# Cross attention on Trainium2: the decode sample's scores of all four heads issued together

## The chip, the core and the metric

The kernel runs on one core of a Trainium2 chip. The metric is the device time of one launch in microseconds (us). Three runs of the kernel before took 992.42, 989.74 and 990.02 us; their median is 990.02 us.

Engines are named as in the profile: PE is TensorE's matrix products and PEld its weight loads, DVE is VectorE, ACT is ScalarE, POOL is GpSimd, SP is SyncE, which issues most of the loads.

## The reference, cut to what matters

One step of a two-layer encoder, for a prompt of 256 tokens and a decode sample of 32 tokens that share the weights. Each layer has a mixer, a cross attention into 256 memory tokens, and an MLP. In the cross attention the prompt uses keys and values projected from its memory; the sample uses cached ones. There are four heads of width 256.

```python
def cross_attend(hn, k, v, w_q, q_gain, w_o):
    b, t, _ = hn.shape
    q = rmsnorm((hn @ w_q).reshape(b, t, N_HEADS_X, HEAD_DIM_X), q_gain)
    s = jnp.einsum('bqhd,bkhd->bhqk', q, k) * (HEAD_DIM_X ** -0.5)
    p = jax.nn.softmax(s, axis=-1).astype(v.dtype)
    o = jnp.einsum('bhqk,bkhd->bqhd', p, v)
    return o.reshape(b, t, -1) @ w_o
```

For the sample that is, per head, a product of 32 queries with 256 keys over a width of 256, which is two products over 128 partitions each.

## The kernel before

All 288 tokens (256 of the prompt, 32 of the sample) are kept feature-major: features on partitions, tokens on columns. Weights stream from HBM in chunks of 1024 x 256 (`load_chunk`). SP loads half a chunk into one of four `raw` buffers; ACT (line 145, sometimes DVE, line 143) rounds it to a first part `wh`, and DVE or POOL (line 146) takes the rest `wl`. Each float32 product is then three products of such parts (lines 160 to 162), and a chunk has 48 of them for 288 columns.

`cross` (line 658) handles a layer's cross attention; the list `ORD_X` gives the order in which its steps are written: `s1 s2 s3 s0 v0 v1 S v2 v3`. A step `s` (`scores`, line 666) loads the head's cached keys `cmk` (line 668, two buffers in turn), projects the queries (`gemm2`), normalises them (`xnorm`: a column sum on PE at lines 329 and 330, `rx` on ACT, the query tile `xq` on DVE at line 343), and then issues two products for the sample (line 678): the 32 sample columns of `xq` are the weights, `cmk` moves through, and the result goes into 32 partitions of the bank `xs`, at the head's own group of 32 array columns (`tile_position=(0, 32 * hd)`). Behind them come the prompt's scores `sx` of the same head, their softmax (DVE lines 452 to 461, ACT line 458) and their transposes (line 697). A step `v` (`values`) projects memory values and multiplies them with the probabilities (`pox`). `S` (`sample`, line 718) takes the softmax of `xs` for all four heads at once and multiplies the cached values (line 729): eight products, two per head, again each head in its own group of 32 array columns, one behind the other.

The order on each engine is not the order of the text. A scheduler in the framework places every instruction when the kernel is built, by its own estimate of when its operands are ready, and each engine then works in that order. So the sample's two products of a head stand between products of weights that are ready anyway.

At the start POOL fills constants: `mones`, `mtri` and `bmask` are tiles of their own; DVE copies the mask into `smask` (line 272) and makes rounded copies `monesr` and `mtrir` (lines 275, 277) before its first split of the tokens (line 198). `scr` is a pool of scratch tiles, with eight buffers in turn under the tag `f`.

Of the kernel before, what the change touches and what calls it, by code (L numbers as in the profile page):

```python
# [14 lines left out]
P = 128  # L15
# [5 lines left out]
FB = 8  # L21
# [32 lines left out]
def body(ctx: ExitStack, tc: tile.TileContext, i: dict, o: dict):  # L54
# [18 lines left out]
    # four PSUM banks and the attentions' scratch change hands from phase to phase  # L73
# [30 lines left out]
    h = const.tile([P, KT, T], F32, name="h")  # L104

# [8 lines left out]
    # the array's clock rises after some microseconds of work, which can go by before the first data are there  # L114
# [5 lines left out]
    def load_chunk(ap, w=CW, split=2, before=None):  # L120
        # before: called with each row tile in turn, whose weights are then loaded on their own
        nk = KT // split
        ws = []
        for s in range(split):
            raw = wraw.tile([P, nk, w], F32, tag="raw", name="raw")
            if before is None:
                nc.sync.dma_start(out=raw, in_=ap[:, s * nk:(s + 1) * nk, :])
            nq = min(nk, NQ) if split > 1 else nk
            step = min(nq, R.step) if before is None else 1
            for k in range(0, nk, step):  # L130
                if k % nq == 0:
                    wh = wspl.tile([P, nq, w], F32R, tag="wh", name="wh")
                    wl = wspl.tile([P, nq, w], F32R, tag="wl", name="wl")
                    ws += [(wh[:, j, :], wl[:, j, :]) for j in range(nq)]
                r, src = slice(k % nq, k % nq + step), raw[:, k:k + step, :]
                if before is not None:
                    nc.sync.dma_start(out=src, in_=ap[:, s * nk + k:s * nk + k + 1, :])
                    before(s * nk + k)
                R.count += 1
                e = nc.gpsimd if R.count % R.pool_every == 0 and before is None else dve  # L140
                with ahead(HPS):
                    if R.dve_every and R.count % R.dve_every == 0 and before is None:
                        dve.tensor_copy(wh[:, r, :], src)
                    else:
                        act(wh[:, r, :], src, AF.Copy)  # L145
                    e.tensor_tensor(wl[:, r, :], src, wh[:, r, :].bitcast(F32), ALU.subtract)  # L146
        return ws
# [6 lines left out]
    def held():  # L154
        # products kept for later, when the engine would have nothing else to do
        return tc.issue_after(R.after) if R.after is not None else ExitStack()

    def mm3(out, lh, ll, rh, rl, first, last):
        # a float32 product from exact float32r parts
        mm(out, lh, rh, start=first, stop=False)  # L160
        mm(out, lh, rl, start=False, stop=False)  # L161
        return mm(out, ll, rh, start=False, stop=last)  # L162

    def gemm(tiles, ws, xh, xl, n=T, steps=GO):
        # the chunk's output tiles advance together, so that its first weights are free early
        for k0, k1 in zip((0,) + steps, steps + (KT,)):
            for out, cols in tiles:
                for k in range(k0, k1):
                    wh, wl = ws[k]
                    last_mm[0] = mm3(out, wh[:, cols], wl[:, cols], xh[:, k, 0:n], xl[:, k, 0:n],  # L170
                                     k == 0, k == KT - 1)
# [15 lines left out]
    class Norm:  # L187
        # (x * gain) in two exact parts, and the rows' 1 / rms, which commutes with the projection
# [11 lines left out]
        def rms(self, pool=()):  # L200
            # the squares of the row tiles in pool are summed by the Pool engine
            sums = {}
            for k in range(KT):
                hk, on = h[:, k, :], k in pool
                if on not in sums:
                    sq = sums[on] = scr.tile([P, T], F32, tag="ssum", name="ssum", bufs=2)
                else:
                    sq = scr.tile([P, T], F32, tag="f", bufs=FB, name="sq")
                if on:
                    nc.gpsimd.tensor_tensor(sq, hk, hk, ALU.mult)  # L210
                else:
                    act(sq, hk, AF.Square)
                if sq is not sums[on]:
                    (nc.gpsimd if on else dve).tensor_tensor(sums[on], sums[on], sq, ALU.add)
            ps = bank(R.m, "ps_rs")
            for n, on in enumerate(sums):
                mm(ps[:, 0:T], ones, sums[on], start=n == 0, stop=n == len(sums) - 1)
            rs = scr.tile([P, T], F32, tag="rs", name="rs")
            rstd_of(ps[:, 0:T], T, 1.0 / 1024, rs)
            return self.xh, self.xl, rs  # L220
# [9 lines left out]
    mones = const.tile([P, P], F32, name="mones")  # L230
    nc.gpsimd.memset(mones, -1.0)
# [8 lines left out]
    # -1 where key' >= key, for the suffix sums of the stick-breaking weights  # L240
    mtri = const.tile([P, P], F32, name="mtri")
    nc.gpsimd.affine_select(mtri, mones, pattern=[[-1, P]], compare_op=ALU.is_ge, fill=0.0,
                            base=0, channel_multiplier=1)
    # causal mask of the forgetting attention: prompt (last key tile) and sample (packed queries)
    bmask = const.tile([P, NP_], F32, name="bmask")
# [27 lines left out]
    # float32r holds 0 and 1 exactly  # L273
    mtrir = const.tile([P, P], F32R, name="mtrir")
    dve.tensor_copy(mtrir, mtri)
    monesr = const.tile([P, P], F32R, name="monesr")
    dve.tensor_copy(monesr, mones)
# [4 lines left out]
    # gains of the query-key norms; the queries' carry the attention scale, and a zero for the other head  # L282
# [40 lines left out]
    def sum_parts(ps, sel, sq, n):  # L323
        # column sums of float32 squares, exactly split in two float32r parts
        sh = scr.tile([P, T], F32R, tag="f", bufs=FB, name="sh")
        dve.tensor_copy(sh[:, 0:n], sq[:, 0:n])
        sl = scr.tile([P, T], F32R, tag="f", bufs=FB, name="sl")
        (nc.gpsimd if HNP else dve).tensor_tensor(sl[:, 0:n], sq[:, 0:n], sh[:, 0:n].bitcast(F32), ALU.subtract)
        mm(ps[:, 0:n], sel, sh[:, 0:n], start=True, stop=False)
        mm(ps[:, 0:n], sel, sl[:, 0:n], start=False, stop=True)  # L330
# [113 lines left out]
    def softmax_rows(s, bias, pr, ntile):  # L444
        # s: list of (scores, bias, probabilities) of 128 queries each; rows are normalised in place
# [17 lines left out]
    def pv_prompt(po, par, p, vt, pt0, pt1):  # L463
        # po: the pair's output features on partitions, prompt queries on columns
# [25 lines left out]
    def attend_ab(kind, g, qz, kT, vt, ck, cv, oh, ol, b1, b0, bsmp):  # L490
        kt0 = 4 * kind + 2 * g
        # sample: 4 heads x 32 queries on the partitions
# [54 lines left out]
    def softplus(zs, w, a):  # L547
        # max(z, 0) + ln(1 + exp(-|z|)); a list of score tiles side by side in w and a
# [13 lines left out]
    def below_diag(x, pattern):  # L562
        # keeps key < query: key on the partitions, query in the last pattern dimension
# [3 lines left out]
    def attend_c(g, qz, kT, vt, ck, cv, oh, ol):  # L567
        kt0 = 2 * g
        k_ = dict(start=False, skip_group_check=True)
        for p in range(2):  # L570
            # key tile 0: both heads' 256 queries; key tile 1: both heads' last 128 queries
# [45 lines left out]
        # sample: 4 heads x 32 queries on the columns, three key tiles  # L617
# [40 lines left out]
    def cross(layer, xh, xl, rs, mk, mh, ml):  # L658
        oh = spp.tile([P, KT, T], F32R, tag="sp", name="oh")
        ol = spp.tile([P, KT, T], F32R, tag="sp", name="ol")  # L660
        ss = bank(R.o, "xs")
# [4 lines left out]
        def scores(hd):  # L666
            cmk = R.ph.tile([P, 2, NP_], F32, tag="ck", name="cmk", bufs=2)
# [9 lines left out]
            for d in range(2):  # L677
                mm(ss[32 * hd:32 * hd + 32, 0:NP_], q[:, d, NP_:T], cmk[:, d, :], start=d == 0, stop=d == 1,  # L678
                   tile_position=(0, 32 * hd))
# [37 lines left out]
        # sample: 4 heads x 32 queries on the partitions  # L717
        def sample():
            pr = scr.tile([P, T], F32, tag="f", bufs=FB, name="prxs")
# [72 lines left out]
    # forget gates; the negated running sums go through DRAM to be read by all partitions  # L792
# [118 lines left out]
def _feat(a, np):  # L911
    # [tokens, features] -> [partition, feature tile, token]
# [4 lines left out]
def _tok(a, np):  # L917
    # [tokens, features] -> [partition, token tile, feature]
# [4 lines left out]
def _chunks(w, np):  # L923
    # [K, N] -> [N/256, 128, K/128, 256]
# [4 lines left out]
def _layout(x, np):  # L929
# [10 lines left out]
    # one row per query: the clipped-relative-position bias of its keys  # L940
# [21 lines left out]
    # [layer, out chunk, quarter, 128, 8, 256]  # L962
# [54 lines left out]
```

## Time and profile before

| | |
|---|---|
| runs | 992.42, 989.74, 990.02 us, median 990.02 |
| profiled execution, first to last instruction | 987.5 us |
| what the median has beyond that span | 2.5 us |
| PE, DVE, ACT, POOL busy | 976.4, 686.6, 541.3, 243.2 us |

The profile is one execution. Its own time by the clock of the runs is not listed beside its span; at the median, 2.5 us would lie around the span. Times of a row are counted from the span's first instruction. Matmuls overlap each other in the records: one that takes 0.29 us by its row starts 0.13 us behind the one before, so how much of PE's time a product costs is read from the starts of its neighbours.

### The profile page before, as it was taken

Reading aid. Unit: us, or ns where it says so; the run is one execution under the profiler, and the core shown is the slowest. Engines: PE = TensorE matmul, PEld = TensorE weight load, DVE = VectorE, ACT = ScalarE, POOL = GpSimd, SP = SyncE. Lnnn points to the kernel's source line nnn. Section 1 sums busy time; section 2 is a strip of 40 time slices with the busy share of each in tenths; the row PEclk is TensorE's granted clock in tenths of the full one; section 3 lists DMA queues with packets and bytes.
Section 4 is the critical chain, followed back from the end, with each engine's and each line's share of the span. In section 5 each row is a group of like instructions: output and inputs, shape, how many; then the busy total and the mean of one; then the engine's idle time right before and its main releaser. Section 6 shows DMA issues by size and latency. Waiting matters only on the chain.

```text
span 987.5 us, 19363 instructions
## 1 busy us (share of the span) xinstructions
PE 976.4 (99%) x7276; PEld 935.3 (95%) x7276; DVE 686.6 (70%) x1460; ACT 541.3 (55%) x1272; POOL 243.2 (25%) x267
## 2 busy tenths in 40 slices
PE   8999999999999999999999999999999999999998
PEld 8998888998999999999999888889999999999998
DVE  8778878678677767776786555668897766464643
ACT  5667566545456645454555657755454565453532
POOL 4311562211112211222122232233333211111111
PEclk8999999999999999999999999999999999999999
DMA  8554454654555555555565434246444455555552
GB/s 272 190 174 147 143 167 160 192 170 131 166 168 169 169 165 161 169 170 160 167 208 188 143 119 142 96 145 204 153 129 149 157 166 166 163 164 171 169 167 75
DMA packets 50702, 160.03 MB, mean 162 GB/s; under 512 B 6296, under 2 KB 12968, under 8 KB 50352
## 3 DMA queue, kind: packets, MB, share of 16 engines
q1 hardware_dynamic: 46864, 148.69, 47.2%
q0 software_dynamic: 2592, 8.92, 2.4%
q10 hardware_dynamic: 1152, 1.18, 0.4%
q8 instruction: 57, 0.93, 0.4%
q14 instruction: 37, 0.30, 0.1%
HBM read 148.65 MB, written 10.12 MB: 161 GB/s over the span
## 4 chain that ended last, share of the span: by engine, by line
PE 96%; DVE 1%; DMA 1%; ACT 0%; issue 0%; SPq 0%; DVEq 0%
PE g L160 27%; PE g L162 27%; PE g L161 27%; PE po L467 1%; PE xs L678 1%; DMA bsmp<-cd 1%; PE za L467 1%; PE za L584 1%; PE s L522 0%; PE zs L624 0%; PE za L605 0%; PE za L468 0%; PE sx L162 0%; SPq L849 0%; PE sx L161 0%
## 5 line engine op out<-in xcount | busy, mean ns | idle before, releaser
L145 ACT ACTIVATE wh<-raw 128x512 fp32r<-128x512 f32 (+3 forms) x561 | 279.4, 549 | 235.5 <-PE g L161 123.0
L146 DVE TENSOR_TENSOR wl<-raw,wh 128x512 fp32r<-128x512 f32 (+3 forms) x483 | 308.9, 673 | 112.2 <-ACT wh L145 106.3
L146 POOL TENSOR_TENSOR wl<-raw,wh 128x512 fp32r<-128x512 f32 (+2 forms) x141 | 175.0, 1242 | 556.1 <-ACT wh L145 465.6
L161 PE MATMUL g<-xl,wh 128*128 128x288 f32 (+1 forms) x1032 | 304.4, 297 | 2.3 <-DVE xl L198 2.3
L160 PE MATMUL g<-xh,wh 128*128 128x288 f32 (+1 forms) x1032 | 302.8, 298 | 1.1 <-ACT wh L145 0.7
L162 PE MATMUL g<-xh,wl 128*128 128x288 f32 (+1 forms) x1032 | 302.7, 298 | 0.0
L161 PEld LDWEIGHTS g<-xl,wh 128*128 128x128 f32 (+1 forms) x1032 | 193.8, 188 | 4.2 <-DVE xl L198 2.5
L162 PEld LDWEIGHTS g<-xh,wl 128*128 128x128 f32 (+1 forms) x1032 | 193.0, 188 | 3.6 <-issue 2.7
L160 PEld LDWEIGHTS g<-xh,wh 128*128 128x128 f32 (+1 forms) x1032 | 192.5, 188 | 2.7 <-ACT wh L145 0.8
L161 PE MATMUL g<-hl,wh 128*128 128x288 f32 x512 | 150.3, 295 | 0.0
L160 PE MATMUL g<-hh,wh 128*128 128x288 f32 x512 | 149.0, 295 | 0.0
L162 PE MATMUL g<-hh,wl 128*128 128x288 f32 x512 | 148.6, 294 | 0.0
L161 PEld LDWEIGHTS g<-hl,wh 128*128 128x128 f32 x512 | 96.1, 188 | 0.0
L162 PEld LDWEIGHTS g<-hh,wl 128*128 128x128 f32 x512 | 95.8, 188 | 0.0
L160 PEld LDWEIGHTS g<-hh,wh 128*128 128x128 f32 x512 | 95.4, 188 | 0.0
L161 PE MATMUL g<-ol,wh 128*128 128x288 f32 x256 | 75.0, 295 | 0.0
L160 PE MATMUL g<-oh,wh 128*128 128x288 f32 x256 | 73.9, 296 | 0.6 <-ACT oh L486 0.6
L162 PE MATMUL g<-oh,wl 128*128 128x288 f32 x256 | 73.9, 296 | 0.0
L774 DVE TENSOR_TENSOR h<-h,g 128x288 f32<-128x288 f32 x64 | 28.8, 449 | 29.0 <-PE g L162 28.9
L160 PEld LDWEIGHTS g<-oh,wh 128*128 128x128 f32 x256 | 47.4, 188 | 1.0 <-ACT oh L486 0.8
L162 PEld LDWEIGHTS g<-oh,wl 128*128 128x128 f32 x256 | 47.7, 188 | 0.6 <-issue 0.6
L161 PEld LDWEIGHTS g<-ol,wh 128*128 128x128 f32 x256 | 48.1, 188 | 0.0
(322 smaller groups left out, 1561.9 us busy)
## 6 DMA issues: line engine op xcount, KB each, us to landing
raw<-in_w_up_dram SPq DMA_DIRECT2D x64, 512.0 KB, 3.8
raw<-in_w_down_dram SPq DMA_DIRECT2D x64, 512.0 KB, 3.8
raw<-in_w_kv_dram SPq DMA_DIRECT2D x32, 512.0 KB, 3.9
raw<-in_sb_w_dram SPq DMA_DIRECT2D x24, 512.0 KB, 4.4
raw<-in_ab_w_dram SPq DMA_DIRECT2D x22, 512.0 KB, 4.9
raw<-in_w_q_dram SPq DMA_DIRECT2D x16, 512.0 KB, 4.5
raw<-in_w_o_dram SPq DMA_DIRECT2D x16, 512.0 KB, 4.1
raw<-in_ab_wo_dram SPq DMA_DIRECT2D x8, 512.0 KB, 4.1
```

The source lines that it names most:

```text
L145: act(wh[:, r, :], src, AF.Copy)
L146: e.tensor_tensor(wl[:, r, :], src, wh[:, r, :].bitcast(F32), ALU.subtract)
L160: mm(out, lh, rh, start=first, stop=False)
L161: mm(out, lh, rl, start=False, stop=False)
L162: return mm(out, ll, rh, start=False, stop=last)
L467: mm(dst[:, 0:NP_], vt[:, 0, cols], pt0, start=True, stop=False)
L584: mm(za2, x[:, 0:P], y, start=f_, stop=False, skip_group_check=True)
L678: mm(ss[32 * hd:32 * hd + 32, 0:NP_], q[:, d, NP_:T], cmk[:, d, :], start=d == 0, stop=d == 1, tile_position=(0, 32 * hd))
L774: dve.tensor_tensor(h[:, kt, :], h[:, kt, :], ps[:, 0:T], ALU.add)
```

## The change

`scores` no longer issues the sample's products. It copies the 32 sample columns of the head's query on POOL into `qsm`, a tile that holds all four heads. The cached keys have four buffers, so that all heads' keys stay. `sample` then issues the eight products, first half of all heads, then second half. The bank `xs` is taken there.

The two float32 constants `mones` and `mtri` and the mask `bmask` become scratch tiles, to make room; the later uses of `mones` and `mtri` read the rounded copies, which hold the same values. The many other lines of the diff only take comments away.

```diff
-    mones = const.tile([P, P], F32, name="mones")
-    nc.gpsimd.memset(mones, -1.0)
+    mones_ = scr.tile([P, T], F32, tag="f", bufs=FB, name="mones")[:, 0:P]
+    nc.gpsimd.memset(mones_, -1.0)
...
-    mtri = const.tile([P, P], F32, name="mtri")
+    mtri_ = scr.tile([P, T], F32, tag="f", bufs=FB, name="mtri")[:, 0:P]
...
-    bmask = const.tile([P, NP_], F32, name="bmask")
+    bmask = scr.tile([P, T], F32, tag="f", bufs=FB, name="bmask")[:, 0:NP_]
...
-    dve.tensor_copy(mtrir, mtri)
+    dve.tensor_copy(mtrir, mtri_)
+    mtri = mtrir.bitcast(F32)
...
     def cross(layer, xh, xl, rs, mk, mh, ml):
         oh = spp.tile([P, KT, T], F32R, tag="sp", name="oh")
         ol = spp.tile([P, KT, T], F32R, tag="sp", name="ol")
-        ss = bank(R.o, "xs")
+        qsm = R.ph.tile([P, 4, 2, NS], F32, tag="qsm", name="qsm")
+        cmks = {}
...
         def scores(hd):
-            cmk = R.ph.tile([P, 2, NP_], F32, tag="ck", name="cmk", bufs=2)
+            cmk = cmks[hd] = R.ph.tile([P, 2, NP_], F32, tag="ck", name="cmk", bufs=4)
...
             xnorm(t, T, xg[:, layer, :], q)
-            for d in range(2):
-                mm(ss[32 * hd:32 * hd + 32, 0:NP_], q[:, d, NP_:T], cmk[:, d, :], start=d == 0, stop=d == 1,
-                   tile_position=(0, 32 * hd))
+            nc.gpsimd.tensor_copy(qsm[:, hd, :, :], q[:, :, NP_:T])
...
         def sample():
+            ss = bank(R.o, "xs")
+            for d in range(2):
+                for hd in range(4):
+                    mm(ss[32 * hd:32 * hd + 32, 0:NP_], qsm[:, hd, d, :], cmks[hd][:, d, :], start=d == 0, stop=d == 1,
+                       tile_position=(0, 32 * hd))
```

In the changed kernel the copy is line 680, the eight products are line 724, the column sums 331 and 332, the loads of the keys 671. What the built order makes of it:

On PE in layer 0, before the change, around the two calls of head 1, the first head. The tiles `g` are weight products, `cmk_2815` is head 1's cached keys, `xq_2882` its query:

```order
L161 MATMUL g_3083<-xl_2749,wh_3077 128x288
L678 MATMUL xs_2812<-cmk_2815,xq_2882 32x256
L162 MATMUL g_3083<-xh_2748,wl_3078 128x288
L160 MATMUL g_3208<-xh_2748,wh_3197 128x288
L161 MATMUL g_3208<-xl_2749,wh_3197 128x288
L678 MATMUL xs_2812<-cmk_2815,xq_2882 32x256
L162 MATMUL g_3208<-xh_2748,wl_3198 128x288
L329 MATMUL ps_xn_3009<-sh_3015,onesr_244 128x288
```

Each of the 16 calls of the two layers stands alone like this: two to four wide products lie between the two calls of a head, and many more between heads.

On PE in layer 0 after the change, where the sample's scores stand now. `cmk_3190` belongs to head 0, `cmk_2815` to head 1, `cmk_2940` to head 2, `cmk_3065` to head 3; `sx_3276` are the prompt's scores of head 0:

```order
L162 MATMUL g_3414<-wh_3408,ml_1560 128x256
L724 MATMUL xs_3485<-cmk_3190,qsm_2812 32x256
L724 MATMUL xs_3485<-cmk_2815,qsm_2812 32x256
L160 MATMUL sx_3276<-mkh_2288,qh_3277 128x256
L161 MATMUL sx_3276<-mkl_2289,qh_3277 128x256
L724 MATMUL xs_3485<-cmk_2940,qsm_2812 32x256
L724 MATMUL xs_3485<-cmk_3065,qsm_2812 32x256
L724 MATMUL xs_3485<-cmk_3190,qsm_2812 32x256
L724 MATMUL xs_3485<-cmk_2815,qsm_2812 32x256
L724 MATMUL xs_3485<-cmk_2940,qsm_2812 32x256
L724 MATMUL xs_3485<-cmk_3065,qsm_2812 32x256
L160 MATMUL g_3538<-wh_3527,mh_1559 128x256
```

All eight have moved behind the projection of the last head, in two runs. The first of them stands 53 rows behind the last column sum (line 332) of head 0's norm, and waits for POOL's copy of head 0. In layer 1 it is 62 rows, and there heads 0 and 1 stand as a run of two, ten products of `sx` follow, and then the rest, in which `cmk_8963` is head 2, `cmk_9092` head 3, `cmk_9221` head 0, `cmk_8834` head 1, and line 698 transposes the prompt's probabilities:

```order
L162 MATMUL sx_9311<-mkh_8217,ql_9313 128x256
L724 MATMUL xs_9528<-cmk_8963,qsm_8831 32x256
L724 MATMUL xs_9528<-cmk_9092,qsm_8831 32x256
L724 MATMUL xs_9528<-cmk_9221,qsm_8831 32x256
L724 MATMUL xs_9528<-cmk_8834,qsm_8831 32x256
L698 MATMUL ps_px_9212<-ident_117,prx_9199 128x128
L724 MATMUL xs_9528<-cmk_8963,qsm_8831 32x256
L698 MATMUL ps_px_9212<-ident_117,prx_9199 128x128 x3
L724 MATMUL xs_9528<-cmk_9092,qsm_8831 32x256
L160 MATMUL g_9585<-wh_9570,mh_6655 128x256
```

So in layer 1 the eight calls are a run of two, a run of four and two single calls.

On POOL in layer 0 after the change; `wl` are rests of weights, `xq_2882` to `xq_3257` the queries of heads 1, 2, 3 and 0, line 375 issues the output of memory values:

```order
L146 TENSOR_TENSOR wl_3195<-raw_3192,wh_3194 128x1024
L680 COPY qsm_2812<-xq_2882 128x64
L680 COPY qsm_2812<-xq_3007 128x64
L146 TENSOR_TENSOR wl_3409<-raw_3406,wh_3408 128x1024
L680 COPY qsm_2812<-xq_3132 128x64
L375 DMA out_memv_dram<-mv_3327 128x2x256
L680 COPY qsm_2812<-xq_3257 128x64
L375 DMA out_memv_dram<-mv_3412 128x2x256
```

The four copies are new; the other rows stand in the same order as before. In layer 1 the copy of head 0 stands behind a split of 512 columns. On SP the loads of all four heads' keys of a layer now stand together ahead of the layer's query weights, where before two stood there and two among later weights. At the start POOL fills a tile `c` (line 813 before) ahead of the mask's `affine_select` (line 247), where before it came behind it; DVE's order there is the same. Up to the first cross attention PE's order is the same as before.

## Rows read from the trace of the kernel before

**Rows 1.** The page: PE's busy time, and the chain that ended last, by engine.

```profile
PE 976.4 (99%) x7276; PEld 935.3 (95%) x7276; DVE 686.6 (70%) x1460; ACT 541.3 (55%) x1272; POOL 243.2 (25%) x267
...
PE 96%; DVE 1%; DMA 1%; ACT 0%; issue 0%; SPq 0%; DVEq 0%
```

**Rows 2.** Waits of PE over the span: us in total, times, longest us.

```profile
PE g L161 <- DVE xl L198: 2.3, 1, 2.3
...
PE pox L162 <- DVE mvl L181: 0.4, 1, 0.4
```

**Rows 3.** Instructions of line 678: duration in ns (min/median/max), first and last start.

```profile
L678 PE MATMUL xs<-cmk,xq x32: 378/392/404, 218.4 to 730.0; 128*32 128x256 f32 x32
```

**Rows 4.** Timeline of PE, layer 0: start us, us, engine, line, operation, out<-in, count.

```profile
218.00 0.29 PE L160 MATMUL g<-xh,wh 128*128 128x288 f32 x1
218.13 0.29 PE L161 MATMUL g<-xl,wh 128*128 128x288 f32 x1
218.35 0.62 PE L678 MATMUL xs<-cmk,xq 128*32 128x256 f32 x2
...
219.14 0.29 PE L160 MATMUL g<-xh,wh 128*128 128x288 f32 x1
```

**Rows 5.** Timeline of PE: head 0's norm and its first score call, both layers.

```profile
239.92 0.29 PE L330 MATMUL ps_xn<-sl,onesr 128*128 128x288 f32 x1
...
244.87 0.62 PE L678 MATMUL xs<-cmk,xq 128*32 128x256 f32 x2
...
723.44 0.30 PE L330 MATMUL ps_xn<-sl,onesr 128*128 128x288 f32 x1
...
728.53 0.28 PE L160 MATMUL g<-wh,mh 128*128 128x256 f32 x1
728.74 0.62 PE L678 MATMUL xs<-cmk,xq 128*32 128x256 f32 x2
...
729.51 0.28 PE L162 MATMUL g<-wh,ml 128*128 128x256 f32 x1
```

**Rows 6.** Timeline of PE around line 729's eight calls, layer 0.

```profile
264.75 0.28 PE L162 MATMUL g<-wh,ml 128*128 128x256 f32 x1
264.95 1.09 PE L729 MATMUL poxs<-cmv,ptxs 128*32 128x256 f32 x16
...
266.20 0.28 PE L161 MATMUL pox<-pl,mvh 128*128 128x256 f32 x1
```

**Rows 7.** Timeline of DVE: head 0's query, layer 0 and layer 1.

```profile
241.80 0.94 DVE L343 SCALAR_TENSOR_TENSOR xq<-tq,xg,rx 128x288 f32<-128x288 f32 x2
...
725.71 2.19 DVE L343 SCALAR_TENSOR_TENSOR xq<-tq,xg,rx 128x288 f32<-128x288 f32 x2
```

**Rows 8.** Timeline of POOL in the cross stages; in brackets idle time before and its releaser.

```profile
239.82 0.74 POOL L373 DMA_DIRECT2D out_memv_dram<-mv  x1 [1.30 <-DVE prx L461]
...
257.45 2.41 POOL L146 TENSOR_TENSOR wl<-raw,wh 128x1024 fp32r<-128x1024 f32 x1
...
725.84 1.31 POOL L146 TENSOR_TENSOR wl<-raw,wh 128x512 fp32r<-128x512 f32 x1
```

**Rows 9.** Timeline of SP's issues ahead of layer 0's cross attention.

```profile
180.16 0.91 SPq L668 DMA_DIRECT2D cmk<-in_cmkT_dram  x2
184.31 6.15 SPq L127 DMA_DIRECT2D raw<-in_w_q_dram  x3
```

**Rows 10.** Two windows: us, then busy us of PE, PEld, DVE, ACT, POOL, clock, DMA.

```profile
218.00:246.00 28.00, 28.00 (x201) 23.91 (x200) 23.32 (x47) 15.19 (x33) 3.11 (x2) 1.00 0.46 147
701.00:731.00 30.00, 30.00 (x215) 25.51 (x214) 25.84 (x52) 14.55 (x36) 9.90 (x8) 1.00 0.42 138
```

**Rows 11.** Timeline of POOL and DVE at the start.

```profile
4.13 0.54 POOL L813 MEMSET c<- 128x544 f32 x1
...
2.26 0.91 DVE L271 COPY eye<-ident 32x32 f32<-32x32 f32 x4 [0.62 <-POOL ident masks.py:199]
...
4.20 3.39 DVE L272 COPY smask<-bmask 32x32 f32<-32x32 f32 x4 [0.66 <-POOL bmask L247]
```

More of the change, by code (lines that the diff above doesn't have):

```diff
@@ L239, in body @@
     nc.gpsimd.memset(m8[64:128, 1:2], 0.125)
-    mtri = const.tile([P, P], F32, name="mtri")
-    nc.gpsimd.affine_select(mtri, mones, pattern=[[-1, P]], compare_op=ALU.is_ge, fill=0.0,
+    mtri_ = scr.tile([P, T], F32, tag="f", bufs=FB, name="mtri")[:, 0:P]
+    nc.gpsimd.affine_select(mtri_, mones_, pattern=[[-1, P]], compare_op=ALU.is_ge, fill=0.0,
                             base=0, channel_multiplier=1)
-    bmask = const.tile([P, NP_], F32, name="bmask")
+    bmask = scr.tile([P, T], F32, tag="f", bufs=FB, name="bmask")[:, 0:NP_]
     nc.gpsimd.memset(bmask, 0.0)
@@ L274, in body @@
     mtrir = const.tile([P, P], F32R, name="mtrir")
-    dve.tensor_copy(mtrir, mtri)
+    dve.tensor_copy(mtrir, mtri_)
+    mtri = mtrir.bitcast(F32)
     monesr = const.tile([P, P], F32R, name="monesr")
-    dve.tensor_copy(monesr, mones)
+    dve.tensor_copy(monesr, mones_)
+    mones = monesr.bitcast(F32)
     onesr = const.tile([P, P], F32R, name="onesr")
```

## The prediction

> **What bounds the kernel now.** I read the page first: TensorE is busy in 99% of the span and 96% of the chain that ended last runs through it [rows 1]. Then the waits of TensorE over the whole span: the longest is 2.3 us at the start, and in the second cross-attention stage there is one of 0.4 us, at its end [rows 2]. So in the stages that the change touches TensorE is the bound, and what counts is the place that a call takes in its stream, not its duration. That place is read from the starts of the neighbours in the timeline.
>
> One sample-score call (two passes, since line 678 shows 32 instructions for 16 calls [rows 3]): products with 288 columns start every 0.13 us (218.00, 218.13). Between 218.13 and the second product behind the call, 219.14, lie 1.01 us in place of 2 x 0.13 = 0.27, so the call takes 0.74 to 0.75 us [rows 4]. Products with 256 columns start every 0.12 us by the same rate (0.13 x 256/288); around the call at 728.74, the last head of layer 1, 729.51 - 728.53 = 0.98 less 0.24 is again 0.74 [rows 5]. All 16 calls stand alone like these two. A pass in itself is 0.24 (0.62 us for two that end alike, durations 0.38 to 0.40 [rows 3, 4]); the rest, about 0.745 - 2 x 0.24 = 0.27, is idle array before and behind the narrow call.
>
> The trace also has the packed form: line 729 issues eight calls in four column groups in one run. From 264.75 to 266.20 are 1.45 us in place of 0.24, so 1.21 us for 16 passes, where eight separate calls would take 5.96 [rows 6]. Four groups with four passes each cost 0.47 more than one group with two.
>
> **The change, part by part.**
>
> Removed: 16 calls of line 678, each alone between wide products: 16 x 0.745 = 11.9 us of TensorE's stream, all on the path.
>
> Added: the same 16 calls from line 724. The built order decides how many runs they make. In layer 0 there are two: heads 0 and 1, then six calls (2, 3, 0, 1, 2, 3). In layer 1 there are four: heads 0 and 1; heads 2, 3, 0, 1; and two lone calls beside transposes. A run costs by its deepest group: two passes 0.745, four passes 1.21. Layer 0: 0.745 + 1.21 = 1.96. Layer 1: 4 x 0.745 = 2.98. Together 4.9 us. Bounds: at best each layer behaves as one run, 2 x 1.21 = 2.4; at worst no two groups overlap, 16 x 2 x 0.24 = 7.7 of passes plus six runs x 0.27 = 9.3. I take 4.9, since [rows 6] is the same operation with the same shapes. Net so far: 4.9 - 11.9 = -7.0.
>
> The timeline shows the idle array around each narrow call [rows 4]. The Trainium skill, TensorEngine Tiling (Array Packing), Key Properties, says that a change of tiling mode drains the engine while tiles of one mode run independently. It speaks against the split into six runs: read without it the six runs would be passes alone and the sum -8.6, with it -7.0, and the trace agrees with the rule, by the 0.27 us around the call.
>
> Copies on POOL (line 680, eight of 128x64): no such copy is in the trace of before. Nearest are the subtractions of line 146 there: 2.41 us for 1024 columns, 1.31 for 512 [rows 8]; the slope leaves 0.2 of fixed time, so about 0.3 us for 64 as an estimate, at most 1.3. Below nothing it cannot go, as nothing is taken off POOL. TensorE waits only for the copy of head 0, the last. In layer 0 its norm's last product is at 239.92 and the query is finished at 241.80 + 0.94 = 242.74, 2.8 us behind [rows 5, 7]. The first new call stands 53 rows behind that product, at 0.12 a row 6.3 us. So 3.5 us are left for a copy of 0.3 to 1.3. In layer 1: product 723.44, query 727.90, 62 rows or 7.3 us, 2.9 left [rows 5, 7]. Cost nothing; without that cover it would be the copy itself. Behind each copy on POOL stand a weight subtraction or the issue of an output (0.74 [rows 8]); the copy holds them only until its query is there.
>
> Loads: two cache loads per layer move ahead of the query weights. Two of them take 0.91 us at 180.16, and the next weight load goes out only at 184.31 [rows 9], so two more fit. SP's waits for a free cache buffer (line 668) go; but TensorE waits for no weights in these stages [rows 2], so their end gives nothing. What is late next on SP is the buffer that the split has to free, as now.
>
> The split engine DVE: here the saving can come back. All eight calls of a layer lie in 218:246 and 701:731, where DVE is busy 23.32 of 28 and 25.84 of 30 us [rows 10]. Taking 5.96 us out leaves 22.0 and 24.0, so DVE is short by 1.3 and 1.8 us there. It has a lead to spend: the query of 242.74 is used at 244.87 (2.1 us early), that of 727.90 at 728.74 (0.8 us) [rows 5, 7]. So I expect nothing back in layer 0 and 1.8 - 0.8 = 1.0 us in layer 1. Bounds: 0 (the new calls put 1.96 and 2.98 us of TensorE time behind the stretch, and part of DVE's busy time is waiting: two queries take 2.19 at 725.71, 0.94 at 241.80 [rows 7]) and 3.1 without any lead.
>
> The start: three constants move into scratch buffers. DVE and TensorE do the same work in the same order, but POOL fills c (0.54 us) before the mask, so the mask's copies on DVE can begin up to 0.54 later. They end the longest wait of TensorE [rows 2, 11]. Now they take 3.39 us, where four equal copies took 0.91 [rows 11]; they run beside a chain of POOL work whose sum stays the same, so I take 0.0, with bounds 0 to +0.5. The four `f` buffers that the constants hold (the mask `bd` is one already) are read by DVE's first instructions, ahead of its first split, so the ring of eight isn't held up by them.
>
> The slow mask copies beside a busy POOL are the row for a rule of the Trainium skill, SBUF — State Buffer, Summary: rules for kernel authors: where DVE and GpSimd contend, the second to issue blocks until the first is done. The trace agrees (3.39 against 0.91). By it the eight small copies could each hold DVE for their length; I price that with the second rival.
>
> Sum: -11.9 + 4.9 + 1.0 + 0.0 = -6.0 us. Against the profiled execution: 987.5 to 981.5. The runs' median lies 2.5 us above that span, and I carry that over: 990.0 - 6.0 = 984.0.
>
> **Rivals.**
>
> *DVE becomes the bound in the cross stages.* For it: 83 and 86% busy there [rows 10], and more per unit of TensorE time after. Against it: TensorE waits there only once now, and DVE regains time in the stretches behind. Price: 3.1 us shortage, and 8 copies x 0.3 = 2.4 us if each holds DVE, 5.5 in all, so -7.0 + 5.5 = -1.5: 988.5.
>
> *The groups do not overlap.* The new calls alternate groups and four of them carry waits, where line 729's eight follow a single one. Against it: those waits are for loads that landed long before. Price: 9.3 - 11.9 = -2.6: 987.4.
>
> *Slower: POOL's copy arrives late and TensorE stands at the first new call.* POOL works in order; ahead of head 0's copy stand the split of 1024 columns (2.4 us) and the issue of an output (0.74) in layer 0, a split of 512 in layer 1, and all wait for other engines. It decides from 3.5 + 3.5 = 7 us of delay per layer after the query, where the wait eats the saving. A copy that stands a whole weight chunk late (two loads of products, 48 x 0.13 = 6.4 us, beyond the 3.2 of lead, plus its split of 2.4) stops TensorE for 5.6 us a layer: +11.2 - 7.0 = +4.2: 994.2. Against it: what stands ahead was done before the query in the trace (239.82 against 242.74; 727.15 against 727.90 [rows 7, 8]).
>
> **How the numbers follow.** Forecast (4 to 9 us saved) 0.78, DVE as bound 0.11, no overlap 0.06, POOL late 0.05. About 0.3%, 3 us, is what a measurement can tell from no change. Faster: 0.78 and a small part of the two middle cases, 0.82; same 0.13; slower 0.05. Likeliest 984.0. Low end 981.0: one run per layer would give -9.5, and no return from DVE; high end 988.0, between the two middle cases.
>
> **What would show it.** Line 724 has 32 instructions in two and four runs; the place of a run is 0.7 to 0.8, or 1.2 for the six calls. No wait of TensorE on POOL's copy. In the cross stages TensorE may show up to some 2 us of waits on DVE in layer 1; more than that, and the second cause is there. From the mixers and the MLPs nothing should come. The first cross stage should get about 4 us shorter, the second about 2; I am wrong if the first doesn't reach 3 or the second 1, or if the first 15 us move by more than 0.5.

## The result and the profile after

Run beside each other on one chip, the kernel before took 989.88 us (median of 4, 989.23 to 992.42) and the kernel after 983.32 us (median of 4, 982.85 to 984.58): a ratio of 0.993, 95% interval 0.9912 to 0.9948. The forecast was 984.0 us. A second comparison gave 983.91 against 989.83, ratio 0.9928 (0.9902 to 0.9955). Two single runs far above all others, one of experiment 1 (1890.09 us) and one of the kernel before beside experiments 1 to 4 (1492.69 us), are left out of the figures below.

The page of after, to set beside [rows 1], and the waits of TensorE over its span, beside [rows 2]:

```profile
PE 971.2 (99%) x7276; PEld 935.6 (95%) x7276; DVE 680.5 (69%) x1460; ACT 541.6 (55%) x1272; POOL 247.7 (25%) x275
...
PE 97%; DVE 1%; DMA 1%; ACT 0%; issue 0%; SPq 0%; ACTq 0%; DVEq 0%
```

```profile
PE g L161 <- DVE xl L198: 1.5, 1, 1.5
...
PE pox L162 <- DVE mvl L181: 0.5, 1, 0.5
```

The same engine is the bound, and no row has it waiting on POOL's copy. To see where the time left, I measure each cross stage from its norm's first product (`ps_rs`) to the start of its last value product (`pox`). Each row gives the shortest, median and longest duration in ns, then the first and last start in us; first the rows of before (layer 0, layer 1), then of after.

```profile
L217 PE MATMUL ps_rs<-ssum,ones x2: 403/404/404, 204.9 to 205.1; 128*128 128x288 f32 x2
...
L162 PE MATMUL pox<-ph,mvl x16: 278/283/387, 260.7 to 269.3; 128*128 128x256 f32 x16
...
L217 PE MATMUL ps_rs<-ssum,ones x2: 406/406/407, 687.8 to 688.0; 128*128 128x288 f32 x2
...
L162 PE MATMUL pox<-ph,mvl x16: 281/283/388, 744.1 to 753.1; 128*128 128x256 f32 x16
```

```profile
L217 PE MATMUL ps_rs<-ssum,ones x2: 403/404/404, 204.2 to 204.4; 128*128 128x288 f32 x2
...
L162 PE MATMUL pox<-ph,mvl x16: 278/282/387, 255.5 to 264.5; 128*128 128x256 f32 x16
...
L217 PE MATMUL ps_rs<-ssum,ones x2: 406/406/407, 684.6 to 684.8; 128*128 128x288 f32 x2
...
L162 PE MATMUL pox<-ph,mvl x16: 278/283/386, 735.9 to 747.0; 128*128 128x256 f32 x16
```

With such marks the whole span divides as follows (us, by the hundredths of the trace):

| | start | mixer 0 | cross 0 | MLP 0 and norms | mixer 1 | cross 1 | rest | span |
|---|---|---|---|---|---|---|---|---|
| before | 15.09 | 189.77 | 64.39 | 236.95 | 181.56 | 65.34 | 234.39 | 987.50 |
| after | 14.71 | 189.48 | 60.34 | 236.95 | 183.10 | 62.40 | 234.38 | 981.36 |
| change | -0.38 | -0.29 | -4.05 | 0.00 | +1.54 | -2.94 | -0.01 | -6.14 |

The two cross stages get 7.0 us shorter. The second mixer, whose code the change hardly touches, gets 1.5 longer and hides part of it; the start and the first mixer get 0.7 shorter.

The new calls in TensorE's stream, layer 0 (start us, duration us, engine, line, operation, out<-in):

```profile
241.31 0.28 PE L162 MATMUL g<-wh,ml 128*128 128x256 f32 x1
241.52 0.62 PE L724 MATMUL xs<-cmk,qsm 128*32 128x256 f32 x4
...
242.30 0.28 PE L161 MATMUL sx<-mkl,qh 128*128 128x256 f32 x1
242.51 1.06 PE L724 MATMUL xs<-cmk,qsm 128*32 128x256 f32 x12
...
243.72 0.28 PE L162 MATMUL sx<-mkh,ql 128*128 128x256 f32 x1
```

Read as in [rows 4]: 242.30 - 241.31 = 0.99, less two spacings of 0.12, is 0.75 for the run of two calls; 243.72 - 242.30 = 1.42 less 0.24 is 1.18 for the run of six. Together 1.93 (forecast 1.96). Layer 1 has its four runs, also as forecast; the rows of line 698 are transposes:

```profile
722.42 0.29 PE L162 MATMUL g<-wh,ml 128*128 128x256 f32 x1
722.64 0.62 PE L724 MATMUL xs<-cmk,qsm 128*32 128x256 f32 x4
...
723.42 0.28 PE L160 MATMUL sx<-mkh,qh 128*128 128x256 f32 x1
...
724.36 0.28 PE L162 MATMUL sx<-mkh,ql 128*128 128x256 f32 x1
724.57 0.64 PE L724 MATMUL xs<-cmk,qsm 128*32 128x256 f32 x8
725.14 0.33 PE L698 MATMUL ps_px<-ident,prx 128*128 128x128 f32 x1
725.39 0.62 PE L724 MATMUL xs<-cmk,qsm 128*32 128x256 f32 x2
725.95 0.55 PE L698 MATMUL ps_px<-ident,prx 128*128 128x128 f32 x3
726.42 0.62 PE L724 MATMUL xs<-cmk,qsm 128*32 128x256 f32 x2
...
727.20 0.28 PE L161 MATMUL g<-wl,mh 128*128 128x256 f32 x1
```

The first run takes 723.42 - 722.42 = 1.00 less 0.24, which is 0.76. The other three stand between 724.36 and 727.20, the second wide product behind them: 2.84, less 0.24 and four transposes of 0.11 each (what one takes between wide products in experiment 4, 728.63 to 729.66), is 2.16. That is 2.92 in all (forecast 2.98), and 4.85 for both layers.

Where the 1.5 us of the second mixer come from, a table of windows shows (stretch and its length in us, busy us of PE, PEld, DVE, ACT and POOL, then the granted clock as a share of 2.4 GHz, the DMA's share and GB/s):

```profile
654.00:657.40 3.40, 3.40 (x33) 3.07 (x31) 0.88 (x2) 1.01 (x3) 0.34 (x2) 1.00 0.39 139
657.40:658.80 1.40, 1.08 (x13) 0.85 (x11) 0.09 (x1) 0.35 (x2) 0.52 (x1) 1.00 0.24 91
658.80:662.20 3.40, 3.40 (x14) 3.40 (x15) 1.28 (x3) 0.57 (x2) 0.00 (x0) 0.50 0.90 276
662.20:680.00 17.80, 17.80 (x135) 17.80 (x135) 16.03 (x30) 12.04 (x27) 5.29 (x4) 1.00 0.66 221
```

From 658.80 to 662.20 the granted clock is at the lower level, 1.2 GHz: 14 products of 288 columns start 0.24 us apart, where they start 0.13 apart before and behind at 2.4 GHz; 14 x 0.11 = 1.5 us. Ahead of the fall TensorE had the end of an attention: products of 32 columns and a wait of 0.3 us on ACT. The trace of before has no fall there. Whether it belongs to the change, experiments 1 and 4 look at.

### The profile page after: what moved, and what is told of

It reads as the page before. It is cut to its first block, busy times and chain, and to the rows that moved or that the text cites. A ratio compares the mean times of both kernels' runs of the same rounds, so it can differ in the third digit from the quotient of the medians.

```text
span 981.4 us, 19371 instructions
## 1 busy us (share of the span) xinstructions
PE 971.2 (99%) x7276; PEld 935.6 (95%) x7276; DVE 680.5 (69%) x1460; ACT 541.6 (55%) x1272; POOL 247.7 (25%) x275
## 3 DMA queue, kind: packets, MB, share of 16 engines
q10 hardware_dynamic: 1152, 1.18, 0.4%
## 4 chain that ended last, share of the span: by engine, by line
PE 97%; DVE 1%; DMA 1%; ACT 0%; issue 0%; SPq 0%; ACTq 0%; DVEq 0%
PE g L160 28%; PE g L162 27%; PE g L161 27%; PE po L469 1%; PE za L469 1%; PE s L524 1%; PE za L586 1%; DMA raw<-in_w_kv_dram 1%; PE zs L626 0%; PE sx L160 0%; PE za L607 0%; PE sx L162 0%; DMA raw<-in_ab_w_dram 0%; PE pox L162 0%; PE ps_px L698 0%; PE pos L478 0%
## 5 line engine op out<-in xcount | busy, mean ns | idle before, releaser
L146 POOL TENSOR_TENSOR wl<-raw,wh 128x512 fp32r<-128x512 f32 (+2 forms) x141 | 177.0, 1255 | 540.7 <-ACT wh L145 438.3
```

## The experiments

My theory: the gain is what the narrow calls take in TensorE's stream, a switch per run plus the passes of its deepest column group. Rivals: the freed memory and earlier loads bring it; fewer switches alone bring it, without overlap of groups; DVE takes part of it back.

**1. The memory part alone.**

```diff
-            nc.gpsimd.tensor_copy(qsm[:, hd, :, :], q[:, :, NP_:T])
+            for d in range(2):
+                mm(ss[32 * hd:32 * hd + 32, 0:NP_], q[:, d, NP_:T], cmk[:, d, :], start=d == 0, stop=d == 1,
+                   tile_position=(0, 32 * hd))
...
```

> The kernel after, with its constants in scratch and its four cache buffers, but the sample's scores issued head by head straight from the query again, 16 lone calls, and no copy on POOL. Theory (the gain is narrow runs taken out of TensorE's stream): 16 runs x 0.745 = 11.9 us stand in the stream as before, so 989.5 us (989.9 less the 0.3 to 0.4 us that the start gained); each lone run takes 0.74 to 0.76 us in the timeline. Rival memory (the freed buffers and the earlier cache loads bring the gain): 983 to 984 us. Rival split engine (time moved off TensorE would be returned anyway by DVE, so only half counts): 986 to 987 us.

Measured: 991.06 us, ratio to before 1.001 (0.9995 to 1.0026). Cross stages 64.37 and 65.36 us, as in before to 0.03. The memory part brings nothing; the rival falls. Its second mixer took 183.10 us, with the same fall of the clock at the same place as in after, although its scores are issued as in before. So the new calls are not needed for the fall. Its trace is 2.5 us longer than that of before: 1.5 in the second mixer and 2.5 in the first, with a fall of the clock in each, less 1.5 at the start. The expected 989.5 had no falls in it.

**2. Two calls per run, in one group.**

```diff
+            for d in range(2):
+                mm(ss[32 * hd:32 * hd + 32, 0:NP_], qsm[:, hd, d, :], cmk[:, d, :], start=d == 0, stop=d == 1,
+                   tile_position=(0, 32 * hd))
...
-            for d in range(2):
-                for hd in range(4):
-                    mm(ss[32 * hd:32 * hd + 32, 0:NP_], qsm[:, hd, d, :], cmks[hd][:, d, :], start=d == 0, stop=d == 1,
-                       tile_position=(0, 32 * hd))
```

> The kernel after, with the copy on POOL, but both calls of a head issued right behind it: 8 runs of two calls (four passes in one column group) in place of six runs of calls in four groups. Theory: a run of four passes in one group costs as much as the packed run whose deepest group has four, 1.21 us, so 8 x 1.21 = 9.7 in place of 11.9 before: 2.2 us less and the start's 0.3, so 987.3 us. If only the number of runs counts (0.27 each, passes as before): 8 x 0.27 less = 2.2, the same 9.7. Rival memory or copy: 983 to 984. Rival overlap alone (no cost of a switch, only passes of 0.24): no gain against before, 989.6.

Measured: 988.03 us, ratio 0.9984 (0.9974 to 0.9995); cross stages 63.13 and 64.42, together 2.2 us shorter than in before, as expected. That refutes the rivals of memory or copy (983 to 984 us) and of overlap without a cost per run (no gain). It doesn't decide between counting runs and counting the deepest group, which gave the same 9.7 us. One of its runs:

```profile
220.23 0.29 PE L162 MATMUL g<-xh,wl 128*128 128x288 f32 x1
220.45 1.05 PE L683 MATMUL xs<-cmk,qsm 128*32 128x256 f32 x4
...
221.66 0.28 PE L161 MATMUL sx<-mkl,qh 128*128 128x256 f32 x1
```

1.43 less spacings of 0.13 and 0.12 is 1.18 for four passes in one group, the place that twelve passes in four groups took above.

**3. All heads in one column group.**

```diff
-            for d in range(2):
+            dve.memset(ss[:, 0:NP_], 0.0)
+            with tc.high_priority(400):
                 for hd in range(4):
-                    mm(ss[32 * hd:32 * hd + 32, 0:NP_], qsm[:, hd, d, :], cmks[hd][:, d, :], start=d == 0, stop=d == 1,
-                       tile_position=(0, 32 * hd))
+                    for d in range(2):
+                        mm(ss[0:32, 0:NP_], qsm[:, hd, d, :], cmks[hd][:, d, :], start=d == 0, stop=d == 1,
+                           tile_position=(0, 0))
```

`tc.high_priority(400)` raises the block's priority in the scheduler; in the built order its eight calls stand together, one run per layer.

> The kernel after with all eight calls of a layer issued in one run, but all four heads in column group 0, so that no two can overlap; of the sample's cross attention only the last head's scores are kept, the other heads get zeros. Theory with overlap of groups: a run of 16 passes in one group takes 16 x 0.24 + 0.27 = 4.1 us in place of 1.21 for the packed run, 8.2 us for both layers in place of 5.0 in the kernel after: 986.5 us. Rival mode switches only (groups don't overlap in the kernel after either, the gain is fewer switches): one run per layer instead of two and four is 4 x 0.27 = 1.1 us better than the kernel after: 982.2 us.

Measured: 985.95 us, ratio 0.9955 (0.9941 to 0.9969); cross stages 62.22 and 63.49.

```profile
243.20 0.28 PE L162 MATMUL g<-wh,ml 128*128 128x256 f32 x1
243.40 3.64 PE L726 MATMUL xs<-cmk,qsm 128*32 128x256 f32 x16
...
247.20 0.28 PE L161 MATMUL sx<-mkl,qh 128*128 128x256 f32 x1
```

4.00 less 0.24 is 3.76 us for 16 passes in one group. It is one run per layer, fewer than in after, and yet each stage is longer than after's. So overlap of groups counts, and the rival of switches alone falls. From 0.745 for two passes and 3.76 for sixteen: 3.015 / 14 = 0.215 a pass and 0.31 a run; for four passes that gives 1.18, which experiment 2 shows.

**4. One run per layer in four groups, and the kernel after again.**

```diff
-            for d in range(2):
-                for hd in range(4):
+            with tc.high_priority(400):
+                for d in range(2):
+                    for hd in range(4):
```

> The kernel after with the eight calls of each layer issued in one run without wide products between them. Theory: 2 x 1.21 = 2.4 us in place of 5.0 in the kernel after, so 2.6 us less: 980.7 us, and the place of each run 1.2 us in the timeline. Rival split engine (DVE has no time left in the second layer): the second layer gives back up to 1.8 us, 982.5 us. Rival: the run waits for the last head's copy on POOL, which now holds all eight calls: one wait of TensorE on POOL of 0.5 us or more, 981.5 us or later.

Measured: 978.95 us, ratio 0.9886 (0.9865 to 0.9906). Cross stages 59.60 and 60.84.

```profile
719.27 0.28 PE L162 MATMUL g<-wh,ml 128*128 128x256 f32 x1
719.47 1.07 PE L725 MATMUL xs<-cmk,qsm 128*32 128x256 f32 x16
...
720.70 0.28 PE L161 MATMUL sx<-mkl,qh 128*128 128x256 f32 x1
```

The run takes 1.43 - 0.24 = 1.19 us, a third of what the same passes take in one group. Experiment 3 has as many runs, and its stages are 2.62 and 2.65 longer, as 3.76 - 1.19 = 2.57 would have it: that is the overlap of groups by itself. Against after, the first stage gets 0.74 shorter, which is what the runs give (1.93 - 1.19). The second gets 1.56 shorter, where the runs give 1.7; TensorE's one wait there, for the rest `mvl` of memory values from DVE, grew from 0.5 to 0.7. No wait on POOL's copy appears. The stages give 2.3 in all; the medians differ by 4.4. To see which holds, both kernels ran again together:

> The kernel after once more, unchanged, for the fall of the granted clock at 658.8 us that cost 1.5 us in its first trace. If that fall belongs to the change (its alignment), it stands in this trace too, at the same place of the program, and the time is 983 to 984 us. If it comes and goes from execution to execution, the trace may lack it, and an execution without it is near 982 us; the two cross stages come out at 60.3 and 62.4 us either way.

> The kernel with one run of eight calls per layer once more, beside the kernel after on the same chip: by the narrow runs it is 2.3 us below it (0.74 in the first cross stage, 1.56 in the second); by the first comparison (978.95 against 983.3) it would be 4.4. Cross stages 59.6 and 60.8 us.

Measured: after 983.91, with one run per layer 980.95 us (ratio to before 0.9898, 0.9869 to 0.9927), 3.0 apart; cross stages 60.35 and 62.40 against 59.59 and 60.84. The stages repeat to 0.01. In the traces the rest of the difference lies in the first 15 us and the mixers: the same kernel after spent 189.48 us in the first mixer in one trace and 191.91 in the other, 1.5 of it at a fall of the clock and 0.8 at a product that waited for DVE in one trace alone. The fall in the second mixer was there again, a microsecond later behind its stage's start. Here are both kernels' windows around it, after's second trace and then the one-run kernel's first; the clock is the third number from the end:

```profile
658.00:663.00 5.00, 4.69 (x41) 4.12 (x40) 1.84 (x5) 1.58 (x4) 0.56 (x1) 0.95 0.39 106
663.00:668.00 5.00, 5.00 (x30) 5.00 (x29) 4.20 (x10) 4.03 (x10) 0.00 (x0) 0.71 0.95 355
```

```profile
658.00:663.00 5.00, 4.69 (x36) 4.58 (x36) 3.79 (x8) 3.37 (x9) 0.00 (x0) 1.00 0.89 289
663.00:668.00 5.00, 5.00 (x40) 5.00 (x39) 5.00 (x10) 4.22 (x11) 2.54 (x1) 1.00 0.88 322
```

Of the 14 traces of this study nine have the fall, always 157.3 to 158.3 us behind the start of the norm ahead of the mixer, and five lack it: before, experiment 3, this kernel twice and the next. TensorE's products in the second mixer up to there come in the same order in all 14. The last four are all the traces of kernels with one run in either layer; that none of them has the fall is more than I would call chance, but no run here shows a cause. Nor does the program alone decide: each run's mean granted clock is on record, and 1.0, no fall at all, stands for one of four runs of the first kernel of experiment 6 and one of ten of its third form with one operation, while a single fall makes 0.998; both kernels have the fall in their trace. The cause stays open.

**5. The copies on DVE.** This is the kernel of experiment 4 with one line changed.

```diff
-            nc.gpsimd.tensor_copy(qsm[:, hd, :, :], q[:, :, NP_:T])
+            dve.tensor_copy(qsm[:, hd, :, :], q[:, :, NP_:T])
```

> The kernel with one run of eight calls per layer, with the copies of the queries on DVE in place of POOL, some 0.2 us each. If DVE has used up its lead in the second layer, that stage is 0.8 us longer than with the copies on POOL (60.8): 61.6, and 979.8 us in all. If lead is left, nothing: 978.9. If the copies on POOL had held up DVE or the weight split, it is faster than that by up to 1 us.

Measured: 980.05 us, ratio 0.9894 (0.9865 to 0.9923); cross stages 59.51 and 60.58. A copy took 0.18 us there (median; one of the eight 1.97). Moving the copies costs nothing; the stages are even 0.08 and 0.26 shorter than in experiment 4, and the wait for `mvl` is 0.4 in place of 0.7. So DVE seems to have had these 0.7 us a layer to spare, even in the fastest kernel; but its built order moved with the edit, so that is not shown by itself.

**6. More work for DVE, three ways.** First an unused product of each head's query:

```diff
+            jk = scr.tile([P, 2, T], F32, tag="t2", name="jk")
+            dve.tensor_tensor(jk, q, t, ALU.mult)
```

> The kernel after with one more DVE operation of 128x576 for each head of the cross attention (an unused product), about 0.8 us each by twice the 0.45 of a 128x288 one, 3.3 us more per layer. In the trace of after DVE is busy 21.9 of 24.0 us in the first layer's stretch and 26.8 of 27.0 in the second's. Theory (DVE runs on a lead in the second layer, used up by the change): the first cross stage grows by 0 to 1 us, the second by 2 to 3.3 us, 986 us. Rival (DVE still has lead, as the missing give-back suggests): both stages grow by less than 0.5, 983.5 us. Rival (DVE binds in both layers): 3.3 each, 990 us.

Measured: 1001.47 us, ratio 1.0097 (1.0063 to 1.0131), far beyond all three. The operation took 0.76 us, 3.0 a layer, and the cross stages 66.61 and 68.61, 6.3 and 6.2 more than after's. But the edit did more than load DVE: its result comes from the ring `t2` of two buffers, which the queries' projections use, and the scheduler built another order on every engine. Hence a form without a buffer, on a constant that nothing reads any more, once in the first kernel and twice in the second:

```diff
+            dve.tensor_tensor(smask, smask, smask, ALU.max)
```

> The kernel after with one idle DVE operation of 128x288 per head in the cross attention, on a constant that nothing reads any more, so that no buffer is held longer: 4 x 0.45 = 1.8 us more DVE time per layer. Theory (DVE's lead in the second layer is nearly used up): nothing in the first cross stage (60.3), up to 1.8 us in the second (62.4 to 64.2), 984 to 985.8 us. Rival (the lead is used up in both, as the 6.3 us per stage of the earlier experiment suggest): 1.8 or more in each, 987.5 us or more. Rival (what the earlier experiment lost came from the buffer that its operation held): both stages unchanged, 983.8 us.

> The same with two such operations per head, 3.6 us more DVE time per layer, somewhat more than the 3.0 of the earlier experiment, and again no buffer held. If DVE's time is what counted there: 6 us or more in each stage, 996 us or more. If the buffer counted: at most 3.6 less the DVE's idle time in each, 2 and 3.5 us, 989 us, or less.

Measured: 983.72 and 985.93 us (ratios 0.9935, 0.9916 to 0.9953, and 0.995, 0.9933 to 0.9967), cross stages 60.35 and 62.39 in both. With equal stages the medians are 2.2 us apart, which shows what a median alone can tell here. These runs tell nothing of the question, as the row of the first one's operation shows:

```profile
L680 DVE TENSOR_TENSOR smask<-smask x8: 434/450/458, 132.2 to 138.4; 128x288 f32<-128x288 f32 x8
```

All eight ran at 132 to 138 us, in the first mixer: nothing tied them to the cross stage, so the scheduler took them early. The third form reads the query, and so has to stay; again once and twice:

```diff
+            dve.tensor_tensor(smask, q[:, 0, :], q[:, 1, :], ALU.max)
```

> The kernel after with one unused DVE operation of 128x288 per head that reads the finished query, so that it must stand in the cross attention, and that writes a dead constant: 1.8 us more DVE time per layer, no buffer taken from a ring. The built order makes other runs of the eight calls: four and four in the first layer (2 x 0.8 = 1.6 us), six and two in the second (1.2 + 0.75 = 1.95), so that by the runs alone the cross stages would be 60.0 and 61.3 us. Theory (DVE's lead in the second layer is nearly used up, in the first 2 us are idle): 60.0 in the first, 61.3 to 63.1 in the second. Rival (lead in both): 60.0 and 61.3. Rival (DVE binds in both): 61.8 and 63.1 or more.

> The same with two such operations per head, 3.6 us more DVE time per layer, more than the 3.0 of the experiment with the unused product, whose result took a buffer of the ring of two that the queries' projections use. Runs of the eight calls: five and three in the first layer (2.0 us), one in the second (1.2): 60.4 and 60.8 us by the runs alone. If DVE's time was what cost 6.3 us per stage there: 66 and 67 us here. If the buffer did: at most 3.6 less the idle time of DVE, 62 and 64 us, or less. If DVE still has lead: 60.4 and 60.8.

Measured: 987.45 us (ratio 0.9972, 0.9956 to 0.9988) and 990.99 (1.0, 0.9986 to 1.0014): 3.5 and 7.1 above after's 983.9, for 3.6 and 7.2 us of DVE work added over both layers. Cross stages 61.71 and 63.92, then 62.20 and 64.76: against after, 1.4 and 1.5 longer with one operation, 1.9 and 2.4 with two. The output projection behind the first stage loses another 1.6 in both, behind the second with two operations only. The longest waits of TensorE with two operations, two of the first layer and then three of the second:

```profile
PE pox L160 <- ACT ph L180: 1.2, 1, 1.2
PE g L160 <- ACT oh L746: 0.7, 1, 0.7
...
PE pox L160 <- DVE ol L716: 2.3, 1, 2.3
PE g L160 <- ACT oh L746: 0.7, 1, 0.7
PE ps_px L698 <- DVE prx L463: 0.6, 1, 0.6
```

So both layers get longer with DVE work of this size, which is nearer to the rival that has DVE bind in both than to mine, which left the first layer free. But it is not shown that DVE's time is the whole cause, and the medians' rise by about the work added proves nothing: the stages grew by 2.9 and 4.2 us for 3.6 and 7.2 of work, and the rest is the output projections. Their 1.6 us come with the built order: they appear exactly where the transposes of the sample's result (line 742) stand behind the last value product, with one operation as with two; in after ten products stand behind them. The longest wait of the first stage is on ACT, 1.2 us, again with one operation as with two. And the eight calls make fewer runs in layer 1, as the expectations say. So the kernel after may stand close to the edge; how close is open.

More than half of the first form's loss is not DVE's time: it added 3.0 us a layer and cost 17.6 in all, this one 3.6 a layer and 7.1. The ring of two buffers and the built order share that rest; they were not separated.

## Why the prediction was right

*What was removed and added.* 16 x 0.745 = 11.9 us out and 4.85 in (forecast 4.9). Both were read from neighbours' starts, and the experiments confirm the price list behind them, with one mending: 0.215 a pass and 0.31 a run, in place of 0.24 and 0.27, give the place of every run in experiments 2, 3 and 4 to 0.03 us, and the four of layer 1 to 0.07 in all. Where a run has four passes in its deepest group, it makes no difference whether the other groups work too (1.18 and 1.19 us). The Trainium skill, TensorEngine Tiling (Array Packing), Key Properties, has the two sides of this, a drain when the tiling mode changes and tiles of one mode that run independently. The runs agree with both: two calls one behind the other take 1.18 us in place of 2 x 0.745, and sixteen passes 3.76 in one group, 1.19 in four. But the rows show starts, not an idle array: that the 0.31 us are the drain, rather than weight loads that don't run ahead, is not separated here (the first weight load of line 729's run starts with its product, at 264.95; those of wide products start 0.12 us ahead).

*The copies on POOL, the loads.* Nothing, as forecast; a copy took 0.25 us in the median and 0.70 at most (estimate 0.3), and the one thing that waited for it was a weight split on POOL, without a wait of TensorE for weights in either stage:

```profile
L680 POOL COPY qsm<-xq x8: 230/252/698, 216.0 to 720.5; 128x64 f32<-128x64 f32 x8
...
  POOL wl L146: 8.7, 1
```

The 2.4 us priced for copies that hold DVE did not come either: with no copy on POOL (experiment 5) the stages are 0.3 us shorter in all.

*What DVE gives back.* This step failed: 1.0 us in layer 1 was forecast, and the stage shortened by 2.94, nearly all of what the runs gave (5.96 - 2.92 = 3.04). The missing 0.1 is the wait for `mvl` at the stage's end, 0.5 us after and 0.4 before. I had set DVE's busy time against the shorter stretch and let a lead of 0.8 us pay, but not the idle time in which DVE itself was waiting for TensorE. These are the windows of after that answer to [rows 10]:

```profile
217.30:241.30 24.00, 24.00 (x198) 24.00 (x197) 21.86 (x49) 15.14 (x33) 4.27 (x5) 1.00 0.45 150
697.80:724.80 27.00, 27.00 (x222) 26.23 (x224) 26.80 (x56) 15.20 (x37) 11.91 (x11) 1.00 0.41 134
```

In layer 1 DVE is busy 26.8 of 27.0 us, and TensorE does not wait in that stretch. Of the 4.2 us that it had idle in before, 3.0 were waits for TensorE, the first two rows of its waits from 701 to 731 there:

```profile
DVE mx L452 <- PE sx L162: 1.6, 1, 1.6
DVE tq L674 <- PE g L162: 1.4, 2, 1.0
```

Those waits are gone in after. The slow pair of queries [rows 7] is gone too; the query's longest operation was 1765 ns in before and is 514 in after. But others are slow there instead, such as the rests of memory values in layer 1, first in before and then in after:

```profile
L343 DVE SCALAR_TENSOR_TENSOR xq<-tq,xg,rx x16: 503/510/1765, 215.6 to 727.4; 128x288 f32<-128x288 f32 x16
L181 DVE TENSOR_TENSOR mvl<-mv,mvh x4: 678/1315/1986, 727.8 to 749.9; 128x512 fp32r<-128x512 f32 x4
```

```profile
L345 DVE SCALAR_TENSOR_TENSOR xq<-tq,xg,rx x16: 504/507/514, 215.0 to 720.0; 128x288 f32<-128x288 f32 x16
L181 DVE TENSOR_TENSOR mvl<-mv,mvh x4: 691/1980/2041, 717.6 to 743.7; 128x512 fp32r<-128x512 f32 x4
```

What DVE's operations took beyond the median of their kind is 6.4 us in before's stretch of layer 1 and 5.1 in after's, so slow operations explain 1.3 us at most. That the waits, with or without these, made up for the 1.8 us that DVE was short is argued from rows, not tested. Experiment 6 suggests that little more DVE work would have done.

*The start.* It moved by -0.38, outside the bounds of 0 to +0.5. The mask's copies did begin later (4.62 us in place of 4.20), but took 2.22 us in place of 3.39. That is no more than the scatter: the 13 traces with the changed start have 13.58 to 15.43 us, and before's 15.09 lies among them. So 0.0 was right as far as it can be told.

*"From the mixers nothing should come."* Not so in the profiled execution: +1.5 us by the fall of the clock, which experiment 1 showed not to need the new calls. It took the place of the 1.0 that DVE did not take, and the start and the first mixer gave 0.7. So that the sum of -6.0 met the measured -6.1 this closely is luck; the two cross stages alone give -7.0.

*The 2.5 us from span to median.* They are not a fixed cost. In every run on record with its span, the time is 1.65 to 1.77 us above it, so the profiled execution of before was 0.8 us faster than the median.

*Rivals.* DVE as the bound: not in this kernel; 1.8 us more of DVE work a layer lengthened both stages in experiment 6, though with another built order. No overlap of the groups: refuted by experiments 3 and 4. POOL's copy late: no wait of TensorE on it in any trace.

## What to carry to other kernels

Price a narrow product by the place that it takes between its neighbours' starts, not by its record, and then count runs and the depth of the deepest column group, since these set the time: here 0.31 us a run and 0.215 a pass. After packing, look at how many runs the built order really makes; forcing one run per layer gave 2.3 us more in the two stages for one line, and the fastest kernels of this study (978.95 and 980.95 us, and 980.05 with the copies on DVE). An engine's idle time is slack only if it isn't waiting for the engine that you are about to speed up; split it by releaser before you book a give-back.

## What the runs showed of the hardware

Products of 32 columns cost 0.31 us a run and 0.215 a pass of the deepest column group, between wide products at 2.4 GHz; other groups of the same run came at no further time (1.19 us for sixteen passes over four groups, 1.18 for four in one).

The granted clock fell to 1.2 GHz within an otherwise busy program, at the same point of it in nine of 14 traces, behind a stretch of 32-column products with gaps, at 1.5 us a time. With a fall in the first mixer, a wait on DVE there and the start, one kernel's span moved by 2.7 us from trace to trace (981.4 and 984.1 for after), with the cross stages equal to 0.01. A difference of a few microseconds between two single executions of this kernel is therefore read by stage, not by span.
